# A two-layer hybrid decoder trunk on one core: the FFN up-projections turned from weights-still to activations-still

## The chip, the cores and the metric

The kernel runs on one core of one Trainium2 chip. The metric is the device time of one execution in microseconds (us). A core has five engines that run beside each other and meet at semaphores: PE (TensorE, the matmuls), DVE (VectorE), ACT (ScalarE), POOL (GpSimd) and SP (SyncE, which here only issues DMAs). 16 DMA engines move data between HBM, called DRAM in the code, and the on-chip memory. In the profile PEld is the loading of a matmul's still operand (its weights, in the engine's words), which runs beside the matmul before it.

## The reference, cut to what matters

Two post-norm layers over 256 tokens with 2048 channels. Each has a mixer (layer 0: Mamba-2 and block-sparse attention; layer 1: native sparse attention and retention) and a convolutional feed-forward network with 5632 channels. The change is mostly about the latter:

```
def causal_depthwise_conv(x, w, b):            # along the tokens, each channel by itself
    ...
def conv_ffn(x, w_up, conv_w, conv_b, w_down):
    a, u = jnp.split(x @ w_up, 2, axis=-1)     # x: 256 x 2048, w_up: 2048 x 11264
    a = causal_depthwise_conv(a, conv_w, conv_b)   # 3 taps
    return (jax.nn.silu(a) * u) @ w_down       # w_down: 5632 x 2048
...
for layer in range(DEPTH):                     # DEPTH = 2
    mix = even_mixer(h, ...) if layer % 2 == 0 else odd_mixer(h, ...)
    h = layer_norm(DEEPNORM_ALPHA * h + mix, ...)
    h = layer_norm(DEEPNORM_ALPHA * h + conv_ffn(h, ...), ...)
```

All of it is in float32.

## The kernel before

**Three products for one.** A float32 product is made of three in the type fp32r: each operand is split into a rounded part `hi` and the rest `lo`, and hi·hi, hi·lo and lo·hi are summed in PSUM. Weights stream from HBM in slabs of 512 KB (`wraw`, 4 buffers); for each slab ACT writes `whi` and DVE `wlo = wraw - whi` (`Weights.prep`, L125 and L126; 4 buffers each). Slabs are asked for three ahead (`AHEAD`). Activations lie as [channel, hi of 256 tokens | lo of 256 tokens], 512 wide, for each of 16 k-tiles of 128 input channels (`x`, and `A`, `B` for the later ones).

**Two forms of a projection.** `group_b` (weights still): 256 output channels a group; for each k-tile two matmuls with `whi` still and the activations' 512 columns moving, and two with `wlo` still and the 256 `hi` columns moving (L345). Its result has channels on the partitions and tokens along the row, so that a convolution along the tokens is a shifted read. `group_a` (activations still, through `three`, L390 to L392): 512 output channels a group; for each k-tile and each half of the tokens three matmuls, in which 512 columns of weights move. Its result has tokens on the partitions.

**Where the forms are used.** The FFN up-projections are `group_b`: per layer 22 pairs of groups, `a` then `u`, 256 channels each. After a group's last matmul its `evac` takes the result from PSUM (`acc`, 2 buffers): `sum_halves` adds the two 256-column halves (ACT L455, DVE L458); `ev_a` then does the 3-tap convolution (ACT L1187, DVE L1190) and SiLU, `ev_u` multiplies (L1199) and splits the product into hi and lo (L304, L305) for the down-projection. The down-projections, the output projections of the mixers, and the first three groups of the odd mixer (`rv`, `rg`) are `group_a`.

**Around a layer norm.** The first group after a norm starts before the norm is done for all tokens: `head_b` for the FFNs (8 slabs of 768 columns) and `head_a` for the odd mixer (4 slabs of 1024 columns) run matmuls for the first 128 tokens, then the second, and `Norm.at` puts the norm's remaining pieces (turns L283, copies, normalisations) between them at places written in `plan`. The slabs of these heads are prepared earlier into the area that `B` or `A` takes later (`out_rest`).

**Fillers.** Attention and other small steps are queued in `Fill`; `group_a` pops one entry per k-tile, `group_b` one per two, and a number added to the queue is so many empty entries. Instructions go to in-order engine queues; a scheduler sets their order on each engine from the program's order, except where an explicit dependency pins it (`strict_from`, `strict_to`).

In the odd mixer `load_bias` reads the attention bias back from HBM in four DMAs on SP (`tmp<-scr`), each followed by a DVE copy (`nb`, L634), in the middle of its projections; `compressor` runs the matmuls of the compressed branch on eight slabs set in among the others by `CMP`, and `project` (L1080 to L1106) finishes each half of them.

Of the kernel before, what the change touches and what calls it, by code (L numbers as in the profile page):

```python
# [9 lines left out]
F32 = mybir.dt.float32  # L10
# [54 lines left out]
CMP = ((OD_VS, 1), (OD_VS, 5), (OD_VW, 0), (OD_VW, 2), (OD_KS, 0), (OD_KS, 2), (OD_KW, 0), (OD_KW, 2))  # L65
# [111 lines left out]
class Norm:  # L177


    def __init__(self, trunk, idx, stats):  # L180
# [5 lines left out]
        if idx == 3:  # L186
            x = trunk.keep.tile([128, 2, DM], F32, name="x")
            self.gb = [[x[:, i, 512 * c:512 * c + 512] for i in range(2)] for c in range(4)]
            u = trunk.fpool.tile([128, 2, 256], F32, name="u", bufs=1)
            self.D, self.pick = u[:, 0, :128], u[:, 1, :128]  # L190
            trunk.nc.gpsimd.memset(self.pick, 0.0)
            trunk.nc.gpsimd.memset(self.pick[0:1, :], 1.0)
        else:
            self.gb = trunk.row_tiles()
            p = "fill", 0, 0
            self.plan = {("t1", 5): ["turn00", "lo00"], ("t1", 7): ["turn01"], ("norm", 0): ["first00", "first01", "second00", "second01"],
                         ("norm", 1): ["lo01", "shift10", "shift11"]}
            if idx == 1:
                more = {("h0", 2): ["turn10", "lo10", "shift02"], ("h1", 0): ["turn11", "lo11", "shift12", "pump"],
                        ("h1", 1): ["turn02", "lo02", "shift03", "pump"],  # L200
                        ("h1", 2): ["turn12", "lo12", "shift13", "pump"], ("h1", 3): ["pump"],
                        ("on", 5): ["turn03", "lo03"], ("on", 7): ["turn13", "lo13"]}
            else:
                more = {("h0", 5): ["turn10", "lo10"], ("h0", 7): ["turn11", "lo11", "shift02", "shift12"],
                        ("h1", 4): ["turn02", "lo02", "pump"], ("h1", 7): ["turn12", "shift03", "lo12", "pump"],
                        ("lo", 3): ["turn03", "shift13", "lo03", "pump"], ("lo", 6): ["turn13", "lo13", "pump"]}
            self.plan.update(more)
# [84 lines left out]
class Trunk:  # L292
# [15 lines left out]
    def group_b(self, act, evacs, head=None):  # L308

        nc, w = self.nc, self.w  # L310
        slabs = w.of[self.job]
        self.job += 1
        nk = len(act)
        width = w.slabs[slabs[0]][4]
        accs = [self.acc_pool.tile([128, 2, 512], F32, name="acc") for _ in evacs[:2]]
        units = [[a[:, o, :] for o in range(min(width // 128, 2))] for a in accs]
        if len(evacs) == 3:
            units.append([self.ps(), self.ps()])
            accs.append(units[2])
        every = 2 if len(evacs) == 1 else 1  # L320
        s = 0
        k0 = 0
        if head:
            k0 = self.head_b(act, units, slabs, head)
            s += k0
        held = []
        while k0 < nk:
            m = w.slabs[slabs[s]][3]
            hi, lo = w.get(slabs[s])
            s += 1  # L330
            if len(units) == 3 and k0 == nk - 2:
                held = [(k0, hi[:, 0], lo[:, 0])]
                k0 += m
                continue
            for kk in range(m):
                part = held + [(k0 + kk, hi[:, kk], lo[:, kk])]
                held = []
                c = 0
                for unit, evac, whole in zip(units, evacs, accs):
                    for k, h, l in part:  # L340
                        wide = [(acc, h[:, c + 128 * o:c + 128 * o + 128], act[k]) for o, acc in enumerate(unit)]
                        half = [(acc[:, :256], l[:, c + 128 * o:c + 128 * o + 128], act[k][:, :256])
                                for o, acc in enumerate(unit)]
                        for i, (acc, wt, mv) in enumerate(wide + half if k < nk - 1 else half + wide):
                            nc.tensor.matmul(acc, wt, mv, start=(k == 0 and i < len(unit)),  # L345
                                             stop=(k == nk - 1 and i >= len(unit)))
                    if k == nk - 1:
                        evac(whole)
                    c += 128 * len(unit)
                if kk % every == every - 1:  # L350
                    self.fill.pop()
            k0 += m
            self.between(slabs[s - 1])
# [5 lines left out]

    def head_b(self, act, units, own, n):  # L360

        nc, w = self.nc, self.w
        slabs = [w.get(own[k]) for k in range(n)]
        w.limit = len(w.slabs)
        order = [0, 2, 1]

        def half(a, t):
            return a.rearrange("p (j c) -> p j c", j=2)[:, :, t * 128:(t + 1) * 128]

        for t in range(2):  # L370
            for k in range(n):
                for u in order:
                    for o, acc in enumerate(units[u]):
                        c = 256 * u + 128 * o
                        nc.tensor.matmul(half(acc, t), slabs[k][0][:, 0, c:c + 128], half(act[k], t),  # L375
                                         start=(k == 0 and t == 0), stop=False)
# [951 lines left out]
```

## Time and profile before

| | |
|---|---|
| median of 3 runs | 2292.39 us (2289.14 to 2294.61) |
| the profiled execution | 2291.93 us; its span, first to last instruction, 2290.1 us |
| PE busy | 2279.4 us (100%) |
| PEld, DVE, ACT busy | 1964.9 us (86%), 1409.4 us (62%), 1093.0 us (48%) |
| POOL busy | 22.4 us (1%) |
| matmuls of `group_b` (L345) | 1179.8 us with `whi` and 726.3 us with `wlo` |
| HBM read, written | 432.41 MB, 2.11 MB |
| granted PE clock | 0.999 |

Busy times of matmuls overlap, since a matmul begins before the one ahead of it has drained. The cost of a stretch of matmuls is therefore read from starts: from the start of its first to the start of the first one behind it. A row of the timeline gives the start, the time from there to the end of its last instruction, engine, line, operation, tiles (out<-in), shape and count. The idle time that a row of groups lists is that of the engine just before those instructions.

### The profile page before, as it was taken

The numbers are of one execution on the slowest core, as the hardware profiler recorded it, in microseconds if no ns is written. First come the engines' busy times: TensorE is split into PE (matmuls) and PEld (weight loads), VectorE is DVE, ScalarE is ACT, GpSimd is POOL, SyncE is SP. The second block draws the span as 40 slices with busy tenths as digits, with TensorE's granted clock in tenths as the row PEclk, the third lists the DMA queues.
The fourth block names the chain that finished last, engine by engine and source line by source line (L and its number), as shares of the span: only waits on it lengthen the run. The fifth ranks groups of instructions, "written<-read, shape, count | busy, mean of one in ns | idle before, by whom it ended". The sixth has DMA issues, their size and how long they took to land.

```text
span 2290.1 us, 31835 instructions
## 1 busy us (share of the span) xinstructions
PE 2279.4 (100%) x12488; PEld 1964.9 (86%) x12488; DVE 1409.4 (62%) x1911; ACT 1093.0 (48%) x1406; POOL 22.4 (1%) x39
## 2 busy tenths in 40 slices
PE   9999999999999999999999999999999999999998
PEld 9888888888888888888889888889888888888887
DVE  5687667666666665445644577767666666654445
ACT  5555543655555554334343464445555555543332
POOL 0001000000000000000000000000000000000000
PEclk9999999999999999999999999999999999999999
DMA  9654474666666667666456645575666666676664
GB/s 298 191 191 157 157 239 143 202 185 193 190 188 189 189 195 218 194 195 215 161 192 206 221 121 156 186 237 151 190 188 189 187 189 189 191 226 194 194 194 138
DMA packets 128487, 436.62 MB, mean 191 GB/s; under 512 B 14240, under 2 KB 16976, under 8 KB 128208
## 3 DMA queue, kind: packets, MB, share of 16 engines
q1 hardware_dynamic: 128048, 434.05, 60.9%
q8 instruction: 98, 1.61, 0.3%
q10 hardware_dynamic: 288, 0.52, 0.1%
q14 instruction: 53, 0.43, 0.1%
HBM read 432.41 MB, written 2.11 MB: 190 GB/s over the span
## 4 chain that ended last, share of the span: by engine, by line
PE 96%; DMA 1%; DVE 1%; ACT 1%; issue 0%; SPq 0%; POOL 0%; DVEq 0%; ACTq 0%; POOLq 0%
PE acc L345 56%; PE acc L390 11%; PE acc L391 11%; PE acc L392 11%; PE ps L392 1%; PE ps L390 1%; PE ps L391 1%; PE ps L714 1%; DMA wraw<-in_od_in 1%; PE acc L375 1%; PE ps L345 0%; PE ps L283 0%; DVE wlo L126 0%; PE ps L665 0%; DMA tmp<-scr 0%; PE ps L375 0%
## 5 line engine op out<-in xcount | busy, mean ns | idle before, releaser
L126 DVE TENSOR_TENSOR wlo<-wraw,whi 128x1024 fp32r<-128x1024 f32 (+3 forms) x782 | 939.5, 1203 | 642.1 <-ACT whi L125 637.4
L345 PE MATMUL acc<-x,whi 128*128 128x512 f32 x3776 | 1179.8, 398 | 0.0
L125 ACT ACTIVATE whi<-wraw 128x1024 fp32r<-128x1024 f32 (+3 forms) x782 | 813.7, 1041 | 725.2 <-PE acc L392 283.6
L345 PEld LDWEIGHTS acc<-x,wlo 128*128 128x128 f32 x3776 | 692.2, 188 | 156.2 <-issue 0.2
L345 PE MATMUL acc<-x,wlo 128*128 128x256 f32 x3776 | 726.3, 279 | 0.0
L345 PEld LDWEIGHTS acc<-x,whi 128*128 128x128 f32 x3776 | 585.6, 189 | 12.6 <-issue 2.2
L390 PE MATMUL acc<-whi,A 128*128 128x512 f32 x448 | 176.0, 393 | 0.0
L392 PE MATMUL acc<-whi,A 128*128 128x512 f32 x448 | 174.6, 390 | 0.0
L391 PE MATMUL acc<-wlo,A 128*128 128x512 f32 x448 | 174.5, 390 | 0.0
L455 ACT ACTIVATE tmp<-acc 128x512 f32<-128x512 f32 x120 | 71.6, 597 | 211.7 <-PE acc L345 208.3
L390 PE MATMUL acc<-whi,B 128*128 128x512 f32 x388 | 151.0, 389 | 0.0
L392 PE MATMUL acc<-whi,B 128*128 128x512 f32 x388 | 151.0, 389 | 0.0
L391 PE MATMUL acc<-wlo,B 128*128 128x512 f32 x388 | 150.9, 389 | 0.0
L392 PEld LDWEIGHTS acc<-whi,A 128*128 128x128 f32 x448 | 84.1, 188 | 17.8 <-DVE A L305 0.3
L390 PEld LDWEIGHTS acc<-whi,A 128*128 128x128 f32 x448 | 84.1, 188 | 17.2 <-ACT A L304 0.4
L391 PEld LDWEIGHTS acc<-wlo,A 128*128 128x128 f32 x448 | 84.2, 188 | 17.0
L390 PE MATMUL acc<-whi,x 128*128 128x512 f32 (+4 forms) x268 | 92.4, 345 | 0.0
L391 PE MATMUL acc<-wlo,x 128*128 128x512 f32 (+4 forms) x268 | 91.7, 342 | 0.5 <-DVE wlo L126 0.5
L392 PE MATMUL acc<-whi,x 128*128 128x512 f32 (+4 forms) x268 | 91.4, 341 | 0.0
L390 PEld LDWEIGHTS acc<-whi,B 128*128 128x128 f32 x388 | 72.8, 188 | 15.2
L392 PEld LDWEIGHTS acc<-whi,B 128*128 128x128 f32 x388 | 72.8, 188 | 15.1
L391 PEld LDWEIGHTS acc<-wlo,B 128*128 128x128 f32 x388 | 72.8, 188 | 15.1
(290 smaller groups left out, 1557.7 us busy)
## 6 DMA issues: line engine op xcount, KB each, us to landing
wraw<-in_up SPq DMA_DIRECT2D x328, 512.0 KB, 4.0
wraw<-in_down SPq DMA_DIRECT2D x176, 512.0 KB, 3.6
wraw<-in_od_in SPq DMA_DIRECT2D x100, 512.0 KB, 3.8
wraw<-in_ev_in SPq DMA_DIRECT2D x72, 512.0 KB, 3.6
wraw<-in_ev_out SPq DMA_DIRECT2D x32, 512.0 KB, 4.4
wraw<-in_od_out SPq DMA_DIRECT2D x32, 512.0 KB, 4.3
wraw<-in_up SPq DMA_DIRECT2D x32, 384.0 KB, 3.8
wraw<-in_ev_in SPq DMA_DIRECT2D x16, 348.0 KB, 4.4
```

The source lines that it names most:

```text
L125: nc.scalar.activation(hi[:, :n], raw[:, :n], AF.Copy)
L126: nc.vector.tensor_tensor(lo[:, :n], raw[:, :n], hi[:, :n].bitcast(F32), op=OP.subtract)
L345: nc.tensor.matmul(acc, wt, mv, start=(k == 0 and i < len(unit)), stop=(k == nk - 1 and i >= len(unit)))
L375: nc.tensor.matmul(half(acc, t), slabs[k][0][:, 0, c:c + 128], half(act[k], t), start=(k == 0 and t == 0), stop=False)
L390: nc.tensor.matmul(o, xh, wh, start=first, stop=False)
L391: nc.tensor.matmul(o, xh, wl, start=False, stop=False)
L392: nc.tensor.matmul(o, xl, wh, start=False, stop=last)
L455: nc.scalar.activation(t, a[:, :, 256:], AF.Copy, scale=sign)
L714: nc.tensor.matmul(d, a, b, start=(i == 0), stop=(i == len(mms) - 1))
```

## The change

The FFN up-projections become `group_a`: per layer 11 pairs of groups of 512 channels, the first pair as one group of 1024 columns (kind `D`) whose head is `head_a` with 4 slabs, as in the odd mixer; `head_b` goes. The result now has tokens on the partitions, so `turned` brings it back: DVE turns each 32 x 32 block straight out of PSUM (L522), POOL writes the tile to HBM in one DMA (L523) and reads it back in four (L526), and only then do the convolution and the gate run. They are queued 14 entries on in `Fill`, and `behind` ties the first instruction of each to the one ahead of it on its engine, so that it cannot be scheduled earlier. The last gate is flushed 12 slabs into the down-projection.

In the odd mixer, the bias and the rotary table are loaded earlier and on POOL's queue, the eight slabs of the compressed branch have other places, and some fillers are spaced otherwise. At the end of `group_a` with a head, the last two k-tiles are done for the first unit, then for the second.

```
-CMP = ((OD_VS, 1), (OD_VS, 5), (OD_VW, 0), (OD_VW, 2), (OD_KS, 0), (OD_KS, 2), (OD_KW, 0), (OD_KW, 2))
+CMP = ((OD_VS, 1), (OD_VS, 4), (OD_VS, 7), (OD_VW, 1), (OD_VW, 3), (OD_KS, 1), (OD_KS, 3), (OD_KW, 0))
 def ffn_jobs(layer):
-    starts = [c + 256 * j for j in range(FT // 2) for c in (0, FF)]
-    out = [(f"up{layer}", "D", cols(*((c, 256) for c in starts[:3])), KT)]
-    out += [(f"up{layer}", "B", cols((c, 256)), KT) for c in starts[3:]]
+    out = [(f"up{layer}", "D", cols((0, 512), (FF, 512)), KT)]
+    out += [(f"up{layer}", "A", cols((c + 512 * j, 512)), KT) for j in range(1, FF // 512) for c in (0, FF)]
...
+                held.append((k, hi[:, kk], lo[:, kk]))        # group_a
+                if early and k == KT - 2:
+                    continue
                 for n, acc, evac in zip(widths, accs, evacs):
-                    for t in range(2):
-                        self.three(acc[:, t, :n], act[k], t, hi[:, kk, c:c + n], lo[:, kk, c:c + n], k == 0, k == KT - 1)
+                    for i, h, l in held:
+                        for t in range(2):
+                            self.three(acc[:, t, :n], act[i], t, h[:, c:c + n], l[:, c:c + n], i == 0, i == KT - 1)
...
-            at = [(1, 3), (1, 5), (1, 7), (2, 1), (2, 3), (2, 5), (2, 7), (3, 1)]      # out_rest
+            at = [(1, 5), (2, 1), (2, 5), (3, 1)]
...
-        if idx == 1:
-            self.early = self.head_a(self.xk, 2, self.heads[1])
-        if idx == 3:
+        if idx < 3:
+            self.early = self.head_a(self.xk, 2, 4)
+        else:
...
+    def turned(self, pool, acc):
+        nc = self.nc
+        t = pool.tile([128, 4, 256], F32, name="T", bufs=2).rearrange("p a b -> p (a b)")
+        d = self.dram.tile([128, 8, 128], F32, name="turn", bufs=2)
+        for h in range(2):
+            to = t[:, 512 * h:512 * h + 512].rearrange("p (j n t) -> p n j t", j=4, n=4)
+            nc.vector.transpose(to, acc[:, h, :].rearrange("p (n j c) -> p n j c", n=4, j=4))
+        nc.gpsimd.dma_start(d, t.rearrange("p (h x) -> p h x", h=8))
+        x = pool.tile([128, 4, 256], F32, name="T", bufs=2).rearrange("p a b -> p (a b)")
+        for j in range(4):
+            nc.gpsimd.dma_start(x[32 * j:32 * j + 32, :].rearrange("c (h i x) -> c h i x", h=2, i=4),
+                                d.rearrange("(i c) (h j) x -> j c h i x", i=4, h=2)[j])
+        return x.rearrange("p (i n t) -> p n i t", i=8, n=4)
...
+                self.fill.add(28, *self.load_bias(P2, ["tmp", "tmp", "q", "q"], nc.gpsimd))   # odd, behind rv
-                self.load_bias(P2, P2)                                                       # odd, behind kw
-                    self.pair(heads)
+                    self.pair(heads, (2, 1 if i else 3, 1))
-        self.fill.add(4, turn, 5, project)
+        self.fill.add(2, turn, 9, project)
...
             def ev_a(j):
                 def go(acc):
-                    held[j] = c = P.tile([128, 2, 256], F32, name="c", bufs=2)
-                    pad = pads[j % 2]
-                    self.sum_halves(P, pad[:, :, 2:258], acc)
...
+                    x = self.turned(P, acc)
+                    held[j] = c = P.tile([128, 4, 256], F32, name="c")
+                    def conv(b):
+                        pad, o = pads[b], c[:, 2 * b:2 * b + 2, :]
+                        nc.scalar.activation(pad[:, :, 2:258].rearrange("p n (i t) -> p n i t", i=8),
+                                             x[:, 2 * b:2 * b + 2], AF.Copy)
...
+                    self.fill.add(14, *(lambda b=b: self.behind(lambda: conv(b)) for b in range(2)))
             def ev_u(j):
                 def go(acc):
-                    u = P.tile([128, 2, 256], F32, name="u", bufs=1)
-                    self.sum_halves(P, u, acc)
-                    nc.vector.tensor_tensor(u, u, held.pop(j), op=OP.mult)
...
+                    x = self.turned(P, acc)
+                    def gate(b):
...
+                    self.fill.add(14, *(lambda b=b: self.behind(lambda: gate(b)) for b in range(2)))
-            self.out_group(gk, 0, 2 * layer + 1)
+            self.out_group(gk, 0, 2 * layer + 1, drain=12)
```

**PE, in the middle of an FFN up-projection, where one group ends and the next begins.** Before (`acc_6493` and `acc_6589` are two groups, `x_79` the activations; "x2" counts equal rows):

```order
L345 MATMUL acc_6493<-x_79,whi_6496 128x512 x2
L345 MATMUL acc_6493<-x_79,wlo_6497 128x256 x4
L345 MATMUL acc_6493<-x_79,whi_6496 128x512 x2
L345 MATMUL acc_6589<-x_79,whi_6518 128x512 x2
L345 MATMUL acc_6589<-x_79,wlo_6519 128x256 x2
```

And now, where the third `a` group (`acc_4223`) ends and its `u` group (`acc_4395`) begins:

```order
L330 MATMUL acc_4223<-whi_4298,x_79 128x512
L331 MATMUL acc_4223<-wlo_4299,x_79 128x512
L332 MATMUL acc_4223<-whi_4298,x_79 128x512
L330 MATMUL acc_4395<-whi_4316,x_79 128x512
L331 MATMUL acc_4395<-wlo_4317,x_79 128x512
L332 MATMUL acc_4395<-whi_4316,x_79 128x512
```

Two matmuls of 512 columns and two of 256 have become three of 512; the columns are the same, 1536.

**DVE and POOL in the same stage.** DVE before, one `a` and one `u` group (`wlo` is the slabs' work, `fpad` and `u` the sums, `c` the convolution, `A` the split):

```order
L458 TENSOR_TENSOR fpad_3550<-acc,tmp 128x2x256
L126 TENSOR_TENSOR wlo<-wraw,whi 128x1024
L1190 SCALAR_TENSOR_TENSOR c<-fpad_3550,prm,c 128x256 x4
L126 TENSOR_TENSOR wlo<-wraw,whi 128x1024 x3
L458 TENSOR_TENSOR u<-acc,tmp 128x512
L1199 TENSOR_TENSOR u<-u,c 128x512
L126 TENSOR_TENSOR wlo<-wraw,whi 128x1024
L305 TENSOR_TENSOR A<-u,A 128x2x256
```

DVE now, from the slabs ahead of an `a` group's end to the end of the `u` group behind it (`T<-acc` is the turn out of PSUM, `c<-T,c` the gate):

```order
L125 TENSOR_TENSOR wlo<-wraw,whi 128x1024 x7
L1163 SCALAR_TENSOR_TENSOR c<-fpad_3640,prm,c 128x256 x4
L125 TENSOR_TENSOR wlo<-wraw,whi 128x1024
L522 STREAM_TRANSPOSE T<-acc 128x4x4x32
L1163 SCALAR_TENSOR_TENSOR c<-fpad_3641,prm,c 128x256 x4
L522 STREAM_TRANSPOSE T<-acc 128x4x4x32
L125 TENSOR_TENSOR wlo<-wraw,whi 128x1024 x7
L1177 TENSOR_TENSOR c<-T,c 128x512
L125 TENSOR_TENSOR wlo<-wraw,whi 128x1024
L297 TENSOR_TENSOR A<-c,A 128x2x256
L1177 TENSOR_TENSOR c<-T,c 128x512
L522 STREAM_TRANSPOSE T<-acc 128x4x4x32 x2
```

POOL before, around the FFN of layer 0 (`rs` belongs to a norm, `ks` to the odd mixer):

```order
L220 TENSOR_TENSOR rs_3368<-rs_3368,mhalf_227 128x1 x2
L1176 MEMSET fpad0_3549 128x2x2
L1176 MEMSET fpad1_3550 128x2x2
L220 TENSOR_TENSOR rs_9164<-rs_9164,mhalf_227 128x1 x2
L957 MEMSET ks_9729 128x2x16
```

POOL now, from the same place on (each `turn` is one group's tile in HBM):

```order
L1145 MEMSET fpad0_3640 128x2x2
L1145 MEMSET fpad1_3641 128x2x2
L523 DMA turn_3857<-T_3856 128x1024
L526 DMA T_3861<-turn_3857 32x8x128 x4
L523 DMA turn_3880<-T_3879 128x1024
L526 DMA T_3884<-turn_3880 32x8x128 x4
L523 DMA turn_4052<-T_4051 128x1024
L526 DMA T_4056<-turn_4052 32x8x128 x4
```

The convolution of a group stands just ahead of the turn of the next `a` group, and a gate just ahead of the turn of the next `u` group: since the first group adds entries for both its units while it pops as one, the queue stays 30 entries long, and from then on each step runs 29 k-tiles (not 15) behind its group's end; the first convolution runs 13 behind. POOL's queue, empty in this stage before, holds five DMAs for each group.

**DVE in the odd mixer, around the second `project`.** Before (`nb` is the bias, `cv`, `cu` and `k` belong to `project`, `q` is the first query group):

```order
L634 COPY nb<-tmp 128x512 x2
L1112 COPY cv<-ps 128x30
L1113 TENSOR_TENSOR cu<-cv 128x30
L1114 TENSOR_SCALAR cu<-cu 128x30
L1115 TENSOR_TENSOR cu<-cu,cv 128x30
L126 TENSOR_TENSOR wlo<-wraw,whi 128x1024
L1117 TENSOR_SCALAR cu<-cu 128x30
L1118 TENSOR_TENSOR cu<-cu,cv 128x30
L1099 COPY k<-cu 128x2x15 x2
L634 COPY nb<-tmp 128x512
```

And now:

```order
L1081 COPY cv<-ps 128x30
L1082 TENSOR_TENSOR cu<-cv 128x30
L1083 TENSOR_SCALAR cu<-cu 128x30
L1084 TENSOR_TENSOR cu<-cu,cv 128x30
L125 TENSOR_TENSOR wlo<-wraw,whi 128x1024
L1086 TENSOR_SCALAR cu<-cu 128x30
L1087 TENSOR_TENSOR cu<-cu,cv 128x30
L1068 COPY k<-cu 128x2x15 x2
L399 TENSOR_TENSOR kw<-acc,tmp 128x512
```

The copies of the bias are gone from here; they stand some 35 rows earlier, among the `wlo` of the `rg` groups.

More of the change, by code (lines that the diff above doesn't have):

```diff
@@ L305, in split, with group_b @@
         self.nc.vector.tensor_tensor(lo, src, hi.bitcast(F32), op=OP.subtract)
-    def group_b(self, act, evacs, head=None):
+    def group_b(self, act, evac):
         nc, w = self.nc, self.w
@@ L313, in group_b @@
         nk = len(act)
[L314 to L353, printed above, removed]
@@ new lines, in group_b @@
+        acc = self.acc_pool.tile([128, 2, 512], F32, name="acc")
+        m = w.slabs[slabs[0]][3]
+        for k in range(nk):
+            if k % m == 0:
+                hi, lo = w.get(slabs[k // m])
+            wide = [(acc[:, o, :], hi[:, k % m, 128 * o:128 * o + 128], act[k]) for o in range(2)]
+            half = [(acc[:, o, :256], lo[:, k % m, 128 * o:128 * o + 128], act[k][:, :256]) for o in range(2)]
+            for i, (o, wt, mv) in enumerate(wide + half if k < nk - 1 else half + wide):
+                nc.tensor.matmul(o, wt, mv, start=(k == 0 and i < 2), stop=(k == nk - 1 and i >= 2))
+            if k == nk - 1:
+                evac(acc)
+            if k % 2:
+                self.fill.pop()
+            if k % m == m - 1:
+                self.between(slabs[k // m])
@@ L358, in between @@
             self.compress(self.w.get(i + 1))
[L360 to L368, printed above, removed]
-        for t in range(2):
[L371 to L376, printed above, removed]
-                self.turns.at(f"h{t}", k)
-        for k in range(n):
-            for u in order:
-                for o, acc in enumerate(units[u]):
-                    c = 256 * u + 128 * o
-                    nc.tensor.matmul(acc[:, :256], slabs[k][1][:, 0, c:c + 128], act[k][:, :256], start=False, stop=False)
-            self.turns.at("lo", k)
-        self.strict_to()
-        return n
     def three(self, o, a, t, wh, wl, first, last):
@@ L441, in group_a @@
                     self.fill.pop()
+                held = []
                 if early:
@@ L623, in bias_scratch, with behind, load_bias @@
         self.fill.add(8, go)
-    def load_bias(self, pool, tmp_pool):
+    def behind(self, go):
+        ins = self.nc.cur_bb.bb.instructions
+        n = len(ins)
+        go()
+        i = list(ins)[n]
+        last = [j for j in list(ins)[:n] if j.engine == i.engine][-1].name
+        self.tc.add_manual_dep(i, last, mybir.DependencyInfo(
+            mybir.DependencyClass.NoSync, mybir.DependencyReason.DATA), reason="not ahead of its place")
+    def load_bias(self, pool, names, queue, tmp_pool=None):
         nc = self.nc
@@ L779, in even @@
                 nc.sync.dma_start(mask, self.I["c_mask"])
-                self.load_bias(P2, P)
+                for a in self.load_bias(P2, ["tmp"] * 4, nc.sync, P):
+                    a()
                 self.fill.flush()
@@ L966, in odd @@
                 yk = [y[:, k, :] for k in range(KT)]
+                cs = P2.tile([128, 2, 256], F32, name="cs")
+                nc.gpsimd.dma_start(cs, self.I["c_rot"])
+                self.fill.add(28, *self.load_bias(P2, ["tmp", "tmp", "q", "q"], nc.gpsimd))
                 for i in range(2):
```

114 lines of the change are left out of this document (52 added, 62 removed).

## The prediction, made before the changed kernel was run

> **What bounds the kernel now.** First the page: which engine is full.
>
> ```profile
> PE 2279.4 (100%) x12488; PEld 1964.9 (86%) x12488; DVE 1409.4 (62%) x1911; ACT 1093.0 (48%) x1406; POOL 22.4 (1%) x39
> ```
>
> PE is busy for all but some 11 us of the span. Then who made PE wait, the four longest (us in total, times, longest):
>
> ```profile
> PE ps L694 <- DVE z L690: 1.7, 2, 1.5
> PE ps L1103 <- DVE k L1099: 1.4, 1, 1.4
> PE ps L1221 <- DVE pad L761: 1.0, 1, 1.0
> PE acc L391 <- DVE wlo L126: 0.5, 1, 0.5
> ```
>
> None lies in an FFN. So an FFN's time is the number of its matmuls times their spacing, and only a change of spacing, or a new wait, moves it. Next the stages, cut at PE's starts (columns: stretch, its length, busy us of PE, PEld, DVE, ACT, POOL with counts, granted clock, DMA share, GB/s):
>
> ```profile
> 373.30:867.80 494.50, 494.50 (x2891) 434.28 (x2890) 313.07 (x372) 256.08 (x314) 0.76 (x3) 1.00 0.61 186
> 867.80:927.66 59.86, 59.86 (x266) 49.55 (x264) 28.87 (x25) 24.46 (x24) 0.00 (x0) 1.00 0.71 212
> 1108.11:1198.20 90.09, 90.09 (x411) 74.44 (x410) 52.55 (x57) 39.27 (x41) 1.34 (x6) 1.00 0.55 178
> 1198.20:1452.00 253.80, 250.57 (x1620) 221.13 (x1619) 163.42 (x377) 119.33 (x232) 2.77 (x4) 1.00 0.56 175
> 1545.24:2039.76 494.52, 494.52 (x2892) 434.29 (x2891) 313.06 (x372) 256.02 (x314) 0.76 (x3) 1.00 0.61 184
> ```
>
> The first and last are the two up-projections with their heads, the second one group of a down-projection, the third the odd mixer's head, `rv` and both `rg` groups, the fourth the NSA part behind it. Last, the spacing itself, weights still and then activations still (start, length, engine and line):
>
> ```profile
> 702.40 0.63 PE L345 MATMUL acc<-x,whi 128*128 128x512 f32 x2
> 702.87 0.39 PE L345 MATMUL acc<-x,wlo 128*128 128x256 f32 x2
> 703.10 0.62 PE L345 MATMUL acc<-x,whi 128*128 128x512 f32 x2
> ...
> 926.98 0.39 PE L390 MATMUL acc<-whi,B 128*128 128x512 f32 x1
> 927.20 0.39 PE L391 MATMUL acc<-wlo,B 128*128 128x512 f32 x1
> 927.43 0.39 PE L392 MATMUL acc<-whi,B 128*128 128x512 f32 x1
> 927.66 0.39 PE L390 MATMUL acc<-whi,A 128*128 128x512 f32 x1
> ```
>
> From `whi` to the next `whi` 0.70 us pass, for 256 channels of one k-tile; the three matmuls that do as much in the other form take 0.68 us. A 512-column matmul is followed after some 233 ns in the first and 227 ns in the second, and the pair of 256 columns costs 0.23 us, more than the one 512-column matmul that replaces it.
>
> **The change part by part.** I call 1536 columns a step: four matmuls before, three after. An up-projection has 44 x 16 = 704 steps in both forms.
>
> *Matmuls, the main term.* The second stretch is 264 matmuls, 88 steps: 59.86 / 88 = 0.6802 us. The third has the form that the up-projection takes, the same head of 4 slabs and the same 24 turns of the norm between its matmuls, with 4 x 32 = 128 steps. So the changed stage should take 90.09 + (704 - 128) x 0.6802 = 481.9 us, against 494.50 and 494.52: 12.6 us less in each layer, 25.2 us in all. The bounds: 0 (the head then costs what it costs, nothing else), and 31 us if the head's 3 us above 128 x 0.6802 also went, which the 24 turns in it mostly forbid.
>
> The Trainium skill, "TensorE: Matmul & The Clock Gate", section "Back-to-back issue gap", speaks against this: it gives an isolated warm matmul N / 2.4 + 2.5 ns, so that 512 columns cost 215.8 and 256 cost 109.2. By it, an estimate, a step would go from 650.0 to 647.5 ns, and the two layers would gain 3.5 us. The rows have 0.70 and 0.68 us, so I go by the rows; a reason may be that four weight loads a step no longer hide, which the formula leaves out.
>
> *PE at the border of the first group.* The next group's accumulator is free only when DVE has turned the first unit. The last two k-tiles of the other unit cover 12 x 0.227 = 2.7 us. DVE needs the `wlo` it has begun, and two turns of 128 x 512 from PSUM, for which there is no row; nearest are an addition that reads PSUM and a shuffle:
>
> ```profile
> L126 DVE TENSOR_TENSOR wlo<-wraw,whi 128x1024 fp32r<-128x1024 f32 x126 | 154.2, 1224 | 94.8 <-ACT whi L125 94.8
> L458 DVE TENSOR_TENSOR u<-acc,tmp 128x512 f32<-128x512 f32 x15 | 10.4, 692 | 19.1 <-ACT tmp L455 19.1
> L1039 DVE STREAM_SHUFFLE tmp<-k 128x512 f32<-128x512 f32 x4 | 3.0, 742 | 0.0
> L125 ACT ACTIVATE whi<-wraw 128x1024 fp32r<-128x1024 f32 x126 | 133.2, 1057 | 90.1 <-PE acc L345 88.7
> L455 ACT ACTIVATE tmp<-acc 128x512 f32<-128x512 f32 x31 | 18.5, 598 | 59.2 <-PE acc L345 59.2
> ```
>
> 1.22 + 2 x 0.74 = 2.7 at most, none at least; a turn at double price would add 1.5. I take 0.5 us a layer, +1.0.
>
> *DVE and ACT work.* For 512 channels of `a` and `u`, DVE's four sums of 0.69 become four turns of 0.69 to 1.5: at most +3.2 us in 43.5, to which its 63% has room. ACT loses four copies of 0.60 and gains two. Both lie beside PE: `whi` waits for PE to free its buffer (88.7 of its 90.1 us idle in the 350 us of up-projection that these rows cover), so weights stand three slabs ahead, 3 x 2.72 us, less 1.06 + 1.22 to make them: PE has 5.9 us of cover when DVE or ACT is held up. Cost 0.
>
> *The round trip.* Per group 0.5 MB out and 0.5 MB in, the latter in 1024 pieces of 512 bytes, all from POOL's queue, where the stage has nothing now. 46 MB in all. No DMA is issued from POOL in this trace; the nearest rows, all from SP's queue (out<-in, count, KB each, median us from issue to landing):
>
> ```profile
> wraw<-in_up SPq DMA_DIRECT2D x328, 512.0 KB, 4.0
> r<-in_tokens SPq DMA_DIRECT2D x4, 512.0 KB, 5.9
> tmp<-scr SPq DMA_DIRECT2D x8, 256.0 KB, 5.8
> q1 hardware_dynamic: 128048, 434.05, 60.9%
> ```
>
> A write like the first row's, 4.0; a read in many pieces like the third (256 pieces, as many as one of the four reads). If the four overlap, as the weights' DMAs do (one for each 4 steps, 2.79 us, and 4.0 to landing): 4.0 + 5.8 = 9.8 us. If they go one by one: 4.0 + 4 x 5.8 = 27.2. Due are they 13 + 2 = 15 k-tiles, 20 us, behind the first unit's end, less 3 for DVE's turns, and 39.5 us behind all later ones. What waits when they are late is the copy into `fpad` on ACT with all `whi` behind it, and the gate on DVE with all `wlo`. At 9.8 nothing waits; at 27.2 the first convolution of a layer is 3 + 27.2 - 20.4 = 9.8 us late, 3.9 beyond PE's cover. I take the overlap, as the weights' row is the nearest to several DMAs in flight: 0, with +8 for two layers as the other end. The 16 DMA engines, 0.61 busy, get 1 MB more per 21.8 us, 48 GB/s beside 186: at the same efficiency 0.77, room enough. The weights' own slack is larger than their 4.0 us: in the same 350 us `whi` waited for PE, not for DMA.
>
> By the Trainium skill, "DMA: Bandwidth & Descriptors", section "Anatomy of one DMA — SWDGE (gpsimd) path", a DMA from POOL takes 2.0 us and its bytes at 436 GB/s: an estimate of 3.2 + 4 x 2.3 = 12.4 us even one by one, in time for every step. No run shows it yet.
>
> *The norm's head.* Four slabs of 1024 in place of eight of 768: it is the odd mixer's head, in which PE did not wait (third stretch), so it is in the main term. *The end.* The last gates stand at the 25th of 44 k-tiles of the down-projection's first group, the first reader of their result at the 41st, 20 us later: 0.
>
> *The odd mixer.* The waits of L1103 and L694:
>
> ```profile
> 1283.60 0.43 DVE L634 COPY nb<-tmp 128x512 f32<-128x512 f32 x1 [1.27 <-DMA tmp<-scr]
> 1284.74 0.43 DVE L634 COPY nb<-tmp 128x512 f32<-128x512 f32 x1 [0.72 <-DMA tmp<-scr]
> 1287.66 0.60 PE L1103 MATMUL ps<-prm,k 128*128 128x128 f32 x3 [1.40 <-DVE k L1099]
> 1301.38 0.72 PE L694 MATMUL ps<-ident,z 128*128 128x128 f32 x4 [1.45 <-DVE z L690]
> ```
>
> In the first, DVE had stood 2.0 us for the bias's DMAs; those are gone from there, and `project` comes four fillers, 5.6 us, further behind `turn`. The second gets two fillers more, 2.8 us. Both should go: -2.85 (0 to -3.2, the stage's whole idle time). The five DMAs that move to POOL precede the FFN's by hundreds of us; their copies stand 28 k-tiles behind them. Cost 0.
>
> *Sum*, against the profiled execution's 2291.93 (span 2290.1 and 1.8 around it): -25.2 + 1.0 - 2.85 = -27.05, 2264.9. That execution is 0.5 us below the median of the runs, so against the median 2265.3.
>
> **The rivals.**
> 1. *The first convolution of each layer is late.* Its four reads land one by one, beside two groups' chains at once (the first `u` group ends 2.7 us behind the first `a`); later chains, one for each 21.8 us, overlap as taken. 2265 + 8 = 2273 as worked above, up to 2284 if a read takes a quarter as long again. For it: 1024 small pieces; against it: the weights' overlap.
> 2. *POOL's chain is the bound, slower.* Each group's write, its landing and four reads follow each other on POOL, and the chain for one group takes longer than the 21.77 us (32 steps) that PE needs. Then the convolutions fall behind by the difference, 22 times a layer, and ACT and DVE, in order, stop with them. With 27.2 us it is 22 x 5.43 = 119 us a layer: 2265 + 239 = 2504. It decides from 22.4 us on, where 22 x 0.61 eats the 13.5 us that a layer gains. For it: nothing shows what POOL takes to issue 1152 pieces. Against: from the rows 9.8 us.
> 3. *No gain on PE.* The spacing is a matter of the neighbours: 3 x 233 ns is 0.699, a step as before, and only the odd mixer gains: 2289. For it: 233 in L345 is for the same 512 columns. Against: the third stretch, 90.09 us for 128 steps with its head and turns. The skill's formula, 3.5 us on PE, would give 2286, and lies beside this.
>
> **How the numbers follow.** Chances: the sum as worked 0.70 (2261 to 2268: all idle time gone and the head cheaper, against turns at double price), rival 1 0.12, rival 3 0.05, rival 2 0.13. Range: from 2261 to 2284, through rival 1's upper part; beyond it are rivals 2 and 3, 0.18. A measurement here tells 0.2%, 4.6 us, from no change. Faster (under 2287.8) 0.82, the same 0.05, slower 0.13.
>
> **What would show it.** Right: from the head's first matmul to the first of the down-projection 482 us in each layer, starts 227 ns apart; no wait of PE in either FFN but up to 1 us where the first group ends; turns near 0.74 us; the reads landed well ahead of the ACT copy into `fpad`; L1103 and L694 without waits. Wrong: PE waiting for `whi` or `wlo` in the FFN, with ACT waiting for a DMA of `T` (rivals 1 and 2: once a layer, or at each group), or spacing of 233 ns (rival 3).

## The result, and the profile after

The changed kernel takes 2264.23 us (median of 4 runs, 2264.02 to 2266.29) against 2290.89 of the kernel before on the same chip (2289.14 to 2294.61): a ratio of 0.9883, 95% interval 0.9872 to 0.9895, 26.7 us less. The profiled execution took 2264.32 us, its span is 2262.2 us, 27.9 less than before.

The page's line on the engines and its two rows for the new DMAs (KB each, median us from issue to landing):

```profile
PE 2254.3 (100%) x10984; PEld 1894.9 (84%) x10984; DVE 1405.7 (62%) x1901; ACT 1071.9 (47%) x1352; POOL 156.7 (7%) x264
...
turn<-T POOLq DMA_DIRECT2D x44, 512.0 KB, 3.2
T<-turn POOLq DMA_DIRECT2D x176, 128.0 KB, 6.0
```

PE still fills the span, with 1504 matmuls fewer. The stages, cut at the same places as before (stretch, length, busy us of PE, PEld, DVE, ACT, POOL with counts, granted clock, DMA share, GB/s):

```profile
373.43:855.12 481.69, 481.69 (x2139) 398.84 (x2138) 306.89 (x358) 243.08 (x282) 63.55 (x108) 1.00 0.77 236
1095.41:1185.46 90.05, 90.05 (x411) 74.52 (x410) 53.40 (x60) 39.36 (x41) 4.75 (x11) 1.00 0.58 190
1185.46:1437.02 251.56, 250.00 (x1616) 220.06 (x1615) 162.85 (x375) 118.18 (x231) 3.36 (x4) 1.00 0.52 173
1530.79:2012.48 481.69, 481.69 (x2139) 398.84 (x2138) 306.87 (x358) 243.21 (x282) 63.40 (x108) 1.00 0.77 236
```

Each up-projection went from 494.50 and 494.52 to 481.69, together 25.6 us; the NSA part from 253.80 to 251.56. These two make the difference of the spans. The spacing in the middle of an up-projection is 227 ns (timeline of PE):

```profile
700.08 0.39 PE L330 MATMUL acc<-whi,x 128*128 128x512 f32 x1
700.31 0.39 PE L331 MATMUL acc<-wlo,x 128*128 128x512 f32 x1
700.53 0.39 PE L332 MATMUL acc<-whi,x 128*128 128x512 f32 x1
```

Who made PE wait, the four longest (us in total, times, longest), none of them inside an FFN:

```profile
PE ps L1201 <- DVE pad L729: 1.1, 1, 1.1
PE acc L331 <- DVE wlo L125: 0.9, 1, 0.9
PE ps L1056 <- ACT k L1044: 0.6, 1, 0.6
PE ps L234 <- ACT c L231: 0.4, 1, 0.4
```

The second and third of these waits are new and lie in the odd mixer; those of L1103 and L694 (now L1072 and L662) are gone.

Now one group's tile on its way, that of the second `a` group of layer 0, in the timeline of DVE, POOL and ACT, one behind the other:

```profile
442.73 1.31 DVE L522 STREAM_TRANSPOSE T<-acc 128x512 f32<-128x512 f32 x2 [1.13 <-ACT fpad L1155]
...
444.33 0.57 POOL L523 DMA_DIRECT2D turn<-T  x1 [7.31 <-DVE T L522]
448.02 2.41 POOL L526 DMA_DIRECT2D T<-turn  x4 [3.12 <-DMA turn<-T]
...
480.93 0.61 ACT L1155 ACTIVATE fpad<-T 128x512 f32<-128x512 f32 x1
```

Two turns, the write, 3.1 us of POOL waiting for it, four reads issued in 2.41 us one behind the other without waiting for each to land. By the rows of the DMAs the last of them is down some 6 us later, at about 456; ACT's copy comes at 480.93, with no wait. Over all 44 groups the trip from the start of the turns to the last landing took 14.9 us in the median, 20.4 at most, and the copies stood 20.0 us (the first of a layer) and 39.0 us (the median) behind the start of the turns.

### The profile page after: what moved, and what is told of

Same layout as the page of the kernel before. It is cut to its first block, busy times and chain, and to the rows that moved or that the text cites. A ratio compares the mean times of both kernels' runs of the same rounds, so it can differ in the third digit from the quotient of the medians.

```text
span 2262.2 us, 29254 instructions
## 1 busy us (share of the span) xinstructions
PE 2254.3 (100%) x10984; PEld 1894.9 (84%) x10984; DVE 1405.7 (62%) x1901; ACT 1071.9 (47%) x1352; POOL 156.7 (7%) x264
## 4 chain that ended last, share of the span: by engine, by line
PE 97%; DMA 1%; DVE 1%; ACT 0%; issue 0%; POOL 0%; SPq 0%; DVEq 0%; ACTq 0%; POOLq 0%
PE acc L330 24%; PE acc L332 24%; PE acc L331 24%; PE acc L314 16%; DMA wraw<-in_od_in 1%; PE ps L330 1%; PE ps L331 1%; PE ps L332 1%; PE ps L682 1%; PE ps L275 0%; PE ps L633 0%; PE ps L662 0%; DVE wlo L125 0%; ACT whi L124 0%; PE ps L859 0%; PE ps L1201 0%
## 5 line engine op out<-in xcount | busy, mean ns | idle before, releaser
L125 DVE TENSOR_TENSOR wlo<-wraw,whi 128x1024 fp32r<-128x1024 f32 (+2 forms) x782 | 940.1, 1207 | 720.3 <-ACT whi L124 716.1
L124 ACT ACTIVATE whi<-wraw 128x1024 fp32r<-128x1024 f32 (+2 forms) x782 | 817.9, 1047 | 930.9 <-PE acc L332 668.3
L330 PE MATMUL acc<-whi,x 128*128 128x512 f32 (+4 forms) x1644 | 628.0, 382 | 0.0
L331 PE MATMUL acc<-wlo,x 128*128 128x512 f32 (+4 forms) x1644 | 626.8, 381 | 0.9 <-DVE wlo L125 0.9
L332 PE MATMUL acc<-whi,x 128*128 128x512 f32 (+4 forms) x1644 | 626.8, 381 | 0.0
L330 PEld LDWEIGHTS acc<-whi,x 128*128 128x128 f32 x1644 | 308.7, 188 | 59.3 <-ACT V L703 0.7
L331 PEld LDWEIGHTS acc<-wlo,x 128*128 128x128 f32 x1644 | 308.8, 188 | 58.9 <-DVE wlo L125 1.1
L332 PEld LDWEIGHTS acc<-whi,x 128*128 128x128 f32 x1644 | 308.7, 188 | 58.4
L314 PE MATMUL acc<-x,whi 128*128 128x512 f32 x1088 | 349.6, 404 | 0.0
L314 PEld LDWEIGHTS acc<-x,wlo 128*128 128x128 f32 x1088 | 199.6, 188 | 44.7 <-issue 0.2
L314 PE MATMUL acc<-x,wlo 128*128 128x256 f32 x1088 | 210.8, 280 | 0.0
L314 PEld LDWEIGHTS acc<-x,whi 128*128 128x128 f32 x1088 | 169.3, 189 | 4.9 <-issue 2.2
L526 POOL DMA_DIRECT2D T<-turn x176 | 106.0, 631 | 157.3 <-DMA turn<-T 102.9
```

The costliest lines, as they stand in the source:

```text
L124: nc.scalar.activation(hi[:, :n], raw[:, :n], AF.Copy)
L125: nc.vector.tensor_tensor(lo[:, :n], raw[:, :n], hi[:, :n].bitcast(F32), op=OP.subtract)
L314: nc.tensor.matmul(o, wt, mv, start=(k == 0 and i < 2), stop=(k == nk - 1 and i >= 2))
L330: nc.tensor.matmul(o, xh, wh, start=first, stop=False)
L331: nc.tensor.matmul(o, xh, wl, start=False, stop=False)
L332: nc.tensor.matmul(o, xl, wh, start=False, stop=last)
```

## The experiments

**1 and 2. The odd mixer's edits: undone in the changed kernel, and alone in the kernel before.** Undone:

```
-CMP = ((OD_VS, 1), (OD_VS, 4), (OD_VS, 7), (OD_VW, 1), (OD_VW, 3), (OD_KS, 1), (OD_KS, 3), (OD_KW, 0))
+CMP = ((OD_VS, 1), (OD_VS, 5), (OD_VW, 0), (OD_VW, 2), (OD_KS, 0), (OD_KS, 2), (OD_KW, 0), (OD_KW, 2))
...
-                nc.gpsimd.dma_start(cs, self.I["c_rot"])
-                self.fill.add(28, *self.load_bias(P2, ["tmp", "tmp", "q", "q"], nc.gpsimd))
...
+                for a in self.load_bias(P2, ["tmp"] * 4, nc.sync):          # behind kw
+                    a()
...
+                nc.sync.dma_start(cs, self.I["c_rot"])
...
-                    self.pair(heads, (2, 1 if i else 3, 1))
+                    self.pair(heads)
...
-        self.fill.add(2, turn, 9, project)
+        self.fill.add(4, turn, 5, project)
```

> The changed kernel with the odd mixer as it was before (places of the compressed branch's slabs, bias and rotary table on SP's queue in the middle, fillers). Theory (the parts add up, 25.6 us from the two up-projections and 2.3 from the odd mixer): the two waits of L1103 and L694 come back with 1.4 us each, the two new ones (wlo 0.9, k 0.6) go, the up-projections stay at 481.7 us; 2264.2 + 2.3 = 2266.5. Rival (the odd edits pay only because the FFN ahead of them now uses other queues, or they cost something in the FFN): the time stays at 2264.2, or the up-projection's 481.7 moves.

> The kernel before with the odd mixer's edits alone. Theory (parts add up): NSA part 251.6 in place of 253.8 us, up-projections unchanged at 494.5; 2290.9 - 2.3 = 2288.6. Rival (the edits gain only together with the new FFN): 2290.9.

Measured: undone 2263.09 us (2262.73 to 2263.76), 0.9875 of before (0.9861 to 0.9890), so no slower than the whole change; alone 2288.41, 0.9988 (0.9979 to 0.9997) of 2292.05, 0.7 to 4.8 us less. The parts don't add up: alone the edits gain (the NSA part took 250.30 us in run 2's trace, 253.80 before, with the waits of L1103 and L694 gone), beside the new FFN they gain nothing. The NSA part with the edits undone:

```profile
1185.00:1436.33 251.33, 250.80 (x1622) 221.23 (x1620) 163.10 (x377) 119.23 (x232) 2.77 (x4) 1.00 0.54 177
```

And the longest wait of PE that is left at the two places:

```profile
PE ps L662 <- DVE z L658: 0.2, 1, 0.2
```

The waits of 1.40 and 1.45 us did not come back, though DVE still stands for the bias. Its first copy of the bias with the edits undone, behind the first matmul of the stretch in which it lies (timeline of PE and of DVE):

```profile
1234.68 0.63 PE L314 MATMUL acc<-x,whi 128*128 128x512 f32 x2
...
1269.77 0.43 DVE L602 COPY nb<-tmp 128x512 f32<-128x512 f32 x1 [2.42 <-DMA tmp<-scr]
```

And the same start before:

```profile
1247.43 0.63 PE L345 MATMUL acc<-x,whi 128*128 128x512 f32 x2
```

The first copy of the bias starts 35.1 us into the stretch here, 36.2 us before (1283.60 in the prediction's rows), and the last of the four 40.8 and 43.7 us. The waits of before are not the chance of one execution, though: run 9 below changes only matmuls of the FFNs in the kernel before, and its trace has them again (waits of PE):

```profile
PE ps L1103 <- DVE k L1099: 1.7, 1, 1.7
PE ps L694 <- DVE z L690: 1.5, 2, 1.2
```

There, too, the first and the last copy are 7.8 us apart, as against 7.6 before and 5.7 in run 1. So both traces with weights still in the FFN and the old odd mixer have the waits, and the one with the new FFN has not. What makes the bias land sooner there is not shown. Run 1 is not the old mixer to the letter either: it keeps the ties of `behind` on the four copies, which the kernel before has not.

**3. Equal widths next to each other.**

```
-            for i, (o, wt, mv) in enumerate(wide + half if k < nk - 1 else half + wide):
+            for i, (o, wt, mv) in enumerate(wide + half if k % 2 == 0 else half + wide):
```

> The changed kernel; in the groups that keep weights still, every second k-tile takes its two 256-column matmuls first, so that matmuls of equal width stand together and the width changes half as often. A weights-still step costs 697.9 ns where four matmuls at 13.4 ns over their columns' time would cost 693.4. Theory A (the 4.5 ns are the changes of width): about 2 ns less in each of some 1100 steps that are left in this form, 1 to 2.5 us less, 2262 to 2263. Theory B (they belong to the 256-column matmuls themselves, or to the still operand): no change, 2264.2.

Measured: 2266.69 us (2265.98 to 2268.15), 0.9893 of before (0.9876 to 0.9909); 2.5 us above the changed kernel's median, which the intervals don't tell from no change. No gain, so theory A fell. The first stage in this form, here and in the changed kernel:

```profile
53.43:281.23 227.80, 227.07 (x1377) 195.69 (x1375) 164.04 (x292) 120.72 (x180) 8.56 (x8) 1.00 0.55 176
```

```profile
53.60:279.78 226.18, 226.18 (x1376) 196.97 (x1375) 163.81 (x292) 120.92 (x180) 7.38 (x8) 1.00 0.55 176
```

1.6 us more in 288 steps, of which 0.7 are a wait. The number of changes of width is not what costs; four of a width in a row don't bring the 227 ns either.

**4. The trip on SP's queue.**

```
-        nc.gpsimd.dma_start(d, t.rearrange("p (h x) -> p h x", h=8))
+        nc.sync.dma_start(d, t.rearrange("p (h x) -> p h x", h=8))
...
-            nc.gpsimd.dma_start(x[32 * j:32 * j + 32, :]...
+            nc.sync.dma_start(x[32 * j:32 * j + 32, :]...
```

> The changed kernel with the five DMAs of each turn issued from SP's queue, on which the weights' loads wait behind them, in place of POOL's. Theory (the trip is hidden wherever it is issued, since weights stand some 10 us ahead): SP stands 3 to 4 us for the write's landing before the reads, PE's new waits stay under 0.3 us a group, 2264 to 2277. Rival (POOL's queue is what makes the trip free): each group's stand on SP ends in a late slab and PE waits 1 to 4 us in each of 44 groups, 2308 to 2440.

Measured: 2263.76 us (2263.29 to 2264.93), no wait of PE in an FFN. The queue makes no difference here. The reads land sooner from it (KB each, median us to landing):

```profile
turn<-T SPq DMA_DIRECT2D x44, 512.0 KB, 3.2
T<-turn SPq DMA_DIRECT2D x176, 128.0 KB, 3.8
```

**5, 6 and 12. The due place.** The number of empty fillers ahead of the convolution and of the gate, 14, is made 2, 6 and 9:

```
-                    self.fill.add(14, *(lambda b=b: self.behind(lambda: conv(b)) for b in range(2)))
+                    self.fill.add(6, *(lambda b=b: self.behind(lambda: conv(b)) for b in range(2)))
```

> The changed kernel with 2 empty fillers ahead of the convolution and the gate in place of 14, so that both are due 3 to 4 k-tiles (4 to 5.5 us) behind the unit's end. The trip takes turns 1.4 + write 0.75 and its landing 3.2 + four reads issued in 2.4 and landing in 6.0, some 14 us. Theory (the 14 fillers hide the trip; ACT and DVE stand for it when it is late, with the slabs' preparation behind them): 9 to 10 us late, 5.9 of it covered, PE waits about 4 us in each of 44 groups, +176 us, 2440. Rival (the places do not matter, as the weights' slack covers any lateness): 2264.

> The changed kernel with 6 empty fillers in place of 14: due 7 to 8 k-tiles (9.5 to 11 us) behind the unit's end, 3 to 4.5 us before the trip's 14 us are over. Theory: the lateness stays inside PE's 5.9 us of cover, ACT shows waits for the reads, PE none or under 0.5 us a group: 2264 to 2286. Rival (any wait of ACT for the trip reaches PE): 3 to 4.5 us in each of 44 groups, 2396 to 2462.

> The changed kernel with 9 empty fillers in place of 14. With 6 the copy into fpad stood ready 9.5 us behind the start of the turns, the trip took 17 us, ACT waited 7.5 us for it, and PE 3.7 us in all (with its granted clock at half for some 5 us behind the wait, that is what 6 and 2 fillers cost: about 81 us). With 9 the place is 4.1 us later. Theory (PE pays only for what exceeds some 4 us of lateness, and then twice): 13.6 us against a trip of 14 to 15, late by 1 us, covered: 2264 to 2268. Rival (any wait of ACT for the trip reaches PE in part): 1 to 3 us in each of 22 pairs, +22 to +70 us.

Measured: 2344.89, 2345.14 and 2336.82 us, one run each. Both theories missed the sizes. With 2 and with 6 the instructions stand in the same order on every engine, so these are two executions of one program. 14 fillers and 2 steps for each of two groups are 32 entries for the 32 k-tiles in which they are popped, so the queue never empties and a step comes a whole pair later, at 39.0 us; with fewer it empties, and ACT is ready for the copy some 10 us behind the start of the turns (medians 11.2, 10.4 and 9.6), all three nearly alike. The trip then takes 16 to 17 us. Why the scheduler puts the work just there, the trace doesn't tell. Waits with 6 fillers:

```profile
ACT fpad L1155 <- DMA T<-turn: 123.2, 22, 8.2
...
PE acc L330 <- ACT whi L124: 23.9, 14, 2.9
PE acc L331 <- DVE wlo L125: 23.6, 22, 2.5
```

The two stages from the matmul behind the head to the first of the down-projection:

```profile
386.47:890.03 503.56, 482.56 (x2073) 393.76 (x2071) 292.64 (x346) 233.65 (x281) 63.02 (x107) 0.98 0.72 224
1584.40:2086.07 501.67, 483.20 (x2074) 393.69 (x2072) 291.85 (x346) 233.53 (x281) 62.85 (x107) 0.98 0.72 224
```

And PE around one of its waits:

```profile
510.43 0.62 PE L330 MATMUL acc<-whi,x 128*128 128x512 f32 x1 [2.58 <-ACT whi L124]
512.16 0.80 PE L331 MATMUL acc<-wlo,x 128*128 128x512 f32 x1 [1.11 <-DVE wlo L125]
512.76 0.63 PE L332 MATMUL acc<-whi,x 128*128 128x512 f32 x1
513.18 0.63 PE L330 MATMUL acc<-whi,x 128*128 128x512 f32 x1
```

ACT stood for the trip at all 22 copies, 5.6 us each, and PE idled 23.9 + 23.6 = 47.5 us at the two lines, all but some 2 us of it in the FFNs: about 1 us for each of the 44 late copies and gates. Against the changed kernel's 468.8 these stages are 34.8 and 32.9 us longer. PE's idle time in them is 21.0 and 18.5 us (length less PE's busy time, in the rows above); from start to start its waits take 24.1 and 21.7, as each also loses the overlap with the matmul ahead of it. Another 9.1 and 9.2 us are a thing that the prediction and the expectations of runs 5 and 6 had left out: behind the wait the matmuls start 426 ns apart, not 227, for 5 us. The granted clock in three pieces from there:

```profile
507.50:512.50 5.00, 1.31 (x4) 0.52 (x3) 4.47 (x10) 5.00 (x8) 0.00 (x0) 0.82 0.00 0
512.50:517.50 5.00, 5.00 (x13) 3.89 (x13) 4.61 (x6) 1.95 (x4) 0.57 (x1) 0.50 0.77 254
517.50:522.50 5.00, 5.00 (x23) 4.11 (x22) 2.42 (x2) 1.93 (x2) 0.87 (x2) 1.00 0.98 365
```

A wait as long as the first of these left the spacing at 227 ns in the run with 2 fillers:

```profile
909.50 0.50 PE L331 MATMUL acc<-wlo,B 128*128 128x512 f32 x1 [2.59 <-DVE wlo L125]
909.84 0.39 PE L332 MATMUL acc<-whi,B 128*128 128x512 f32 x1
910.07 0.39 PE L330 MATMUL acc<-whi,B 128*128 128x512 f32 x1
```

The Trainium skill, "TensorE: Matmul & The Clock Gate", section "HAM oscillation — how this bites in real kernels", warns of gaps of PE above some 3.4 us, behind which the clock is at half. The half is what the rows have; the limit was lower here: over the three runs, waits of PE that follow each other closely never halved it up to 1.2 us in all, did so sometimes between 1.6 and 2.6, and always from 2.7 us on. The traces' records of the clock show why the length alone does not tell. Each stretch of half clock lasts 3.41 us or 6.83, and within a trace all of them start a whole number of 3.41 us apart. Cut on that grid, a piece at full clock in which PE idled 2.0 us or more was always followed by half clock, one with up to 1.5 us never, and between 1.6 and 1.9 both occurred. The wait of 2.59 us above lies across a border of the grid, 1.82 and 0.76 us; the one of 2.58 lies in one piece, and so does one of 2.01 us in the same run with 2 fillers, which was followed by half clock.

**7. Each read twice.**

```
-        for j in range(4):
+        for j in (0, 1, 2, 3, 0, 1, 2, 3):
```

> The changed kernel with each of the four reads of a turn issued twice: 23 MB and 176 DMAs more, POOL's chain some 2.4 us longer for each group. Theory (POOL's chain takes some 7 us of the 21.8 that a group lasts, and the DMA engines, 0.77 busy, take 0.85): no new wait of PE, 2264 to 2266. Rival (POOL's chain or the DMA engines are near their limit): PE waits in the FFNs, +1 us a group or more, 2308 or more.

**11. No trip at all.** `turned` returns `t`; the write and the reads are gone.

> The changed kernel without the round trip: no write, no reads, the convolution and the gate take the tile that DVE turned block by block (so the channels are in the wrong places; the same work on ACT, DVE and PE). Theory (the trip is hidden entirely): 2264 within 2 us. Rival (the 47 MB on the DMA engines cost the weights or PE something spread over the stage, as a spacing above 226.7 ns): faster by more than 2 us.

Measured: 2264.80 (one run) and 2264.18 us (2262.78 to 2265.45; 0.9874 of before, 0.9860 to 0.9889). The up-projection of layer 0 behind its head, in the changed kernel, with each read twice, and without the trip:

```profile
386.31:855.12 468.81, 468.81 (x2073) 388.17 (x2072) 295.53 (x341) 237.60 (x275) 63.00 (x107) 1.00 0.79 242
```

```profile
386.74:855.54 468.80, 468.80 (x2073) 388.37 (x2072) 296.00 (x341) 237.82 (x275) 112.19 (x191) 1.00 0.95 264
```

```profile
386.19:854.98 468.79, 468.79 (x2074) 388.17 (x2072) 295.21 (x341) 237.60 (x275) 0.21 (x2) 1.00 0.61 195
```

468.8 us with 195, 242 and 264 GB/s, and with a DMA share of 0.61, 0.79 and 0.95. The trip costs nothing, and with the reads doubled it costs nothing in the up-projections either, though the chain is then 25.1 us long in the median, 10 more: from the first read's issue to the last's 9.2 us pass for eight, and 1.7 for four. ACT stood 2.0 and 1.0 us for the first copy of the two layers there, and PE did not wait behind it: so much lateness is covered. One wait of PE, 0.76 us, lies in the down-projection of layer 1, where slabs came late beside the last doubled reads.

**8 and 9. What a matmul costs by width.** Eight: the new form with two matmuls of half the width for one.

```
+                            z = n // 2 if split and 0 < i < KT - 1 else n
+                            for q in range(0, n, z):
-                            self.three(acc[:, t, :n], act[i], t, h[:, c:c + n], ...
+                                self.three(acc[:, t, q:q + z], act[i], t, h[:, c + q:c + q + z], ...
```

Nine: the old form with all matmuls 512 wide.

```
-                        half = [(acc[:, :256], l[:, c + 128 * o:c + 128 * o + 128], act[k][:, :256])
+                        half = [(acc[:, :n], l[:, c + 128 * o:c + 128 * o + 128], act[k][:, :n])       # n = 512
```

> The changed kernel with the 512-column matmuls of 14 of the 16 k-tiles, in all groups of the up-projections but the first pair, each as two of 256 columns with the same still operand: 6 matmuls and 1536 columns a step, 560 steps a layer. Theory A (each matmul costs 13.4 ns besides its columns, 512 / 2.4 + 13.4 = 226.7): 6 x 120 = 720 ns a step, 40 more, 2 x 560 x 0.040 = +45 us, 2309. Theory B (a load of the still operand, 188 ns, does not hide behind 256 columns): 6 x 188 = 1128 ns, +502 us, 2766. Theory C (a half costs what the 256-column matmuls cost with weights still, 116.5): 699 ns, +21 us, 2285.

> The kernel before; in all groups of its up-projections but the first three, the two matmuls of a step with wlo still also take all 512 columns (the product lo x lo is added to the result): a step is 4 x 512 columns with weights still, 656 steps a layer. Theory A (a 512-column matmul costs 233 ns in this form whatever stands beside it, as the alternating order suggests): 932 ns a step in place of 698, 2 x 656 x 0.234 = +307 us, 2598. Theory B (the 6 ns over 226.7 come from 256-column neighbours): 907 ns, +274 us, 2565.

Measured: 2309.22 and 2568.41 us (one run each). The first is theory A to the microsecond; in the second, theory B is within 4 us and A 30 off. Starts in the timeline of PE, eight:

```profile
599.89 0.28 PE L331 MATMUL acc<-wlo,x 128*128 128x256 f32 x1
600.01 0.28 PE L332 MATMUL acc<-whi,x 128*128 128x256 f32 x1
```

and nine (two matmuls a row):

```profile
600.77 0.61 PE L345 MATMUL acc<-x,wlo 128*128 128x512 f32 x2
601.23 0.62 PE L345 MATMUL acc<-x,whi 128*128 128x512 f32 x2
```

Alone among its like, a 256-column matmul takes 120.0 ns and a 512-column one 226.7, whichever operand is still (means over some 3500 and 2500 starts; the prediction's rows had 233 for 512 with weights still). So 256 columns more cost 106.7, and 13.3 ns are left for the matmul itself. Mixed, as in the step of before, the wide ones take 232.8 and the narrow ones 116.1, a step 697.8 where 2 x 226.7 + 2 x 120.0 = 693.4. Of the 17.7 ns that a step gains, 13.3 are the fourth matmul, and 4.4 go with the mixture. Why a mixture costs that stays open; runs 3 and 9 exclude the number of changes and the form. The Trainium skill, "TensorE: Matmul & The Clock Gate", section "Back-to-back issue gap", has 2.5 ns for an isolated matmul where the matmuls of this stream show 13.3; its rate for a column agrees.

**10. The tiles turned by PE.** `turned` copies the two units with ACT and DVE into one tile; ahead of each convolution or gate PE turns four 128 x 128 blocks.

```
+        def take(b):
+            ps = self.ps()
+            for n in range(2):
+                for h in range(2):
+                    nc.tensor.transpose(ps[:, 256 * n + 128 * h:256 * n + 128 * h + 128],
+                                        t[:, h, 256 * b + 128 * n:256 * b + 128 * n + 128], self.ident)
+            return ps.rearrange("p (n x) -> p n x", n=2)
```

> The changed kernel with the chunks turned on PE: ACT and DVE copy each unit out of PSUM, and PE turns it back with eight 128 x 128 transposes for a group just ahead of the convolution or the gate; no HBM trip. Theory (PE is the bound, what is added to it is paid in full): 8 transposes at 0.09 us start to start, 44 groups, +31 us, 2295, the PE gain of the change used up. Rival (transposes fit into gaps of PE): 2264.

Measured: 2303.84 us (2303.41 to 2304.66), 1.0047 of before (1.0030 to 1.0064): slower than the kernel before. 39.6 us over the changed kernel, not 31:

```profile
459.78 0.60 PE L526 MATMUL ps<-ident,T 128*128 128x128 f32 x4
460.14 0.47 PE L330 MATMUL acc<-whi,x 128*128 128x512 f32 x1
460.45 0.39 PE L331 MATMUL acc<-wlo,x 128*128 128x512 f32 x1
```

Four turns take 0.36 us from start to start, and the matmul behind them is 0.31 from the next, some 0.09 more than usual: 0.45 us for four, 88 times, is 39.6. The transposes did not fit into gaps of PE.

## Why the prediction was right, point by point

- *Matmuls, -12.6 us a layer.* Right: 481.69 where 90.09 + 576 x 0.6802 gave 481.9. The reason offered there, four loads of the still operand that no longer hide, fell: in run 8 a load of 191 ns stands ahead of each matmul of 120 ns, the loads overlap one another, and the time is that of theory A. Those 13.3 ns are a price per matmul; whether the loads have a part in the 4.4 ns of the mixture is open.

```profile
L331 PEld LDWEIGHTS acc<-wlo,x 128*128 128x128 f32 x2764 | 528.6, 191 | 14.6 <-DVE wlo L125 0.3
```

- *First group's border, +1.0.* Too much: no wait. A turn of 128 x 512 from PSUM took 0.70 us in the mean, near the 0.74 assumed, and nothing of it showed on PE:

```profile
L522 DVE STREAM_TRANSPOSE T<-acc 128x512 f32<-128x512 f32 x88 | 59.8, 702 | 12.9 <-PE acc L332 7.0 <-ACT fpad L1155 2.3 <-DMA turn<-T 1.7
```

- *DVE and ACT, 0.* Right; 5.9 us of cover was not needed. In run 7 lateness of 2.0 us stayed inside it; in runs 5, 6 and 12 lateness of 5 to 7 us, with the held-up convolution's own work behind it, was already more than it could hold.
- *The round trip, 0.* Right in cost, short in length: 9.8 us were taken from the end of the turns, 13.0 were measured in the median. The write took 3.2 against 4.0; the reads are issued over 1.7 us and land some 6 to 7 us later, and POOL idles 0.5 between. They overlap, as assumed, and 20 and 39 us from the start of the turns were there. The Trainium skill, "DMA: Bandwidth & Descriptors", section "Anatomy of one DMA — SWDGE (gpsimd) path", gave 12.4 us one by one; from the write's issue to the last landing the trace has 12.7 in the median, but put together otherwise: the write is the skill's 3.2, a read takes 6.0 and not 2.3, and four of them overlap.
- *Odd mixer, -2.85.* 253.80 - 251.56 = 2.2 in the two profiles, with both waits gone and two new ones of 0.9 and 0.6. But beside the new FFN the edits are not what does it: run 1 has the same stage at 251.33 us without them. They do gain in the old kernel (run 2: 250.30), where both traces show the waits. So the term was priced in the kernel before and added to a change beside which run 1 has the waits gone without it; that it came out for the whole is in part luck.
- *Sum.* 25.6 and 2.2 make up the 27.9 between the spans, where 27.05 was forecast; between the medians it is 26.7.
- *Rival 1, first convolution late.* Did not happen; the trip of the first `a` group took 14.4 and 14.5 us of 20.0. Its second half, though, was as feared for the `u` group behind it: POOL stood 8.9 us for a write issued just behind four reads, and that trip took 20.3 us, due 37.9. Had the rival come true it would probably have cost more than the 8 us given, since waits of PE of 3.9 us were followed by half clock in runs 5 and 6.

```profile
425.09 0.64 POOL L523 DMA_DIRECT2D turn<-T  x1
434.61 2.41 POOL L526 DMA_DIRECT2D T<-turn  x4 [8.88 <-DMA turn<-T]
```

- *Rival 2, POOL's chain as the bound.* Wrong in kind: it counted the landing of each read into what POOL is held for. POOL waits for the write alone: from the write's issue to the end of the last read's issue it is held 6.2 us of the 21.8 of a group in the median, and with the reads doubled 15.1; a chain of 25 us cost nothing, where 22.4 was said to decide.
- *Rival 3, no gain on PE.* Excluded by the 227 ns; run 9 shows 227 in the old form too, once all matmuls are wide.

## What to carry to other kernels

Where PE is full, count matmuls and not only columns: here each costs 13.3 ns beside its columns, so three wide ones beat two wide and two narrow. Whatever the new layout then needs should go to an idle engine and its queue, with a due place fixed further on than the trip is long (39 us for 15 here); the same turn on PE cost 39.6 us, more than the 25.6 that the form gains, and the trip due at about 10 us cost 73 to 81. A wait of one or two us beside a DMA's landing can go with another part of the same change, so its price should start from zero.

## What the runs showed of the hardware that was not expected

- Half clock (427 ns for 512 columns) came behind waits of PE in stretches of 3.41 or 6.83 us on a grid of 3.41 us: always when PE had idled 2.0 us or more of one piece of the grid, never up to 1.5. Each stretch added 1.5 to 2.9 us beside the wait itself.
- Mixed widths: 232.8 and 116.1 ns where equal ones take 226.7 and 120.0. The narrow ones get cheaper and the wide ones dearer, by more.
- The same four reads landed in 3.8 us from SP's queue and 6.0 from POOL's; from the first issue to the last, eight in a row from POOL took 9.2 us where four took 1.7.
- Loads of the still operand overlapped each other: 191 ns each, every 120 ns.
- DMA engines 0.95 busy (264 GB/s) did not slow the weights enough to be seen on PE in the up-projections (468.8 us in both).
